# Nine matmuls on zeros at the start, the first norm's column sums one step later, and another count for GpSimd's low parts

## The chip, the core and the metric

The kernel runs on one core of one Trainium2 chip. The metric is the device time of one execution in microseconds, as the median of several runs. A profiled execution gives the trace; its span runs from the first to the last instruction.

## The reference

The kernel computes two transformer blocks in f32 on 256 tokens of width 1024. What matters here is the beginning of the first block:

```python
def rms_norm(x, g):
    xf = x.astype(jnp.float32)
    y = xf * lax.rsqrt(jnp.mean(xf * xf, axis=-1, keepdims=True) + EPS)
    return (y * g.astype(jnp.float32)).astype(x.dtype)

h = rms_norm(x, attn_pre_norm)
proj = h @ w_in                  # queries, keys, values of three attentions, and gates
...                              # attentions, gated merge, w_out, residual
x = x + rms_norm(h, attn_post_norm)
h = rms_norm(x, ffn_pre_norm)
h = conv_ffn(h, w_up, conv_w, conv_b, w_down)
x = x + rms_norm(h, ffn_post_norm)
```

A second block of two layers follows: a modulation made from `ada_w`, a state-space branch, a differential attention and an MLP, with a context stream beside it, and a last `rmsnorm`.

## The kernel before

Activations lie transposed: eight tiles `x[k]` of 128 channels by 256 tokens. A weight comes in pieces of 128x1024 f32 (512 KB). `wload` loads a piece into `wr`, ScalarE rounds it to a high part `wh` (L210), and VectorE or GpSimd subtracts to get the low part `wl` (L213). A product is then three matmuls for each of the eight channel tiles: high by high (L230), high by low of the activation (L231), low of the weight by high (L232), so 24 for a piece. In `mmN` (L251 to L253) the activation is the stationary operand. There are seven `wr` buffers, five `wh` and five `wl`; the program has 578 pieces. Which engine makes a low part is decided by a count:

```python
self.nsplit += 1
eng = nc.gpsimd if self.nsplit % self.pool_every == 0 else nc.vector
```

`pool_every` is 4 for the first block and changes by stage (4, 8 or 99). `nsplit` starts at 0.

A planner puts the instructions of VectorE, ScalarE, GpSimd and the load queue in order, by priority among what is ready by its own estimates. TensorE's order is the one in which the program issues its matmuls (`in_order`). `weave` takes one step of the dense work, then one step of each background generator in `bg`.

The first block begins with the loads of piece 1 (on GpSimd's queue), the eight `x[k]`, and pieces 2 to 4, all of the highest priority. `xg` is `x` times `pre_g` (the tile tag is `o`), split into a high half by ScalarE (L391) and a low half by VectorE (L392). The first dense work, `prods_c`, multiplies `xg` instead of the normed `h`, and applies the norm's factor to the products. Its steps are piece 1, piece 2, piece 3, piece 4 (24 matmuls each), the first half of pieces 5 and 6, their second half. Behind the first half it issues four VectorE products (L489) that use `rt`, the norm's factor spread over the partitions. `prods_b` follows and is the first that needs `h`.

In the background `pre_norm` runs. Its first step squares `x` on GpSimd (`sq`, L299) and adds the squares on VectorE (L303). The next step issues the column sums on TensorE (L312: four plain f32 matmuls, two records each) and the factor `rr` with its diagonals `dg` (L272 to L278: VectorE, GpSimd, VectorE). The next issues `spread` (L286) and `rt` (L405), and the last issues the sweep that makes `h`: `hv` (L410) on VectorE, its high half on ScalarE (L256) and its low half on VectorE (L257). `bias_rows` and, later, `heads_c` and `steps_ada` (L916) run beside it.

`norm` has a `wait` argument: so many more steps go by before the column sums are issued. It is 0 in `pre_norm`.

Of the kernel before, what the change touches and what calls it, by code (L numbers as in the profile page):

```python
# [10 lines left out]
F32 = mybir.dt.float32  # L11
# [6 lines left out]
P = 128  # L18
# [80 lines left out]
class Net:  # L99
    def __init__(self, ctx, tc, A, stop=None, x_only=False):  # L100
        self.ctx, self.tc, self.nc, self.A = ctx, tc, tc.nc, A
        self.stop = stop
        p = lambda name, bufs, **k: ctx.enter_context(tc.tile_pool(name=name, bufs=bufs, **k))
        self.cp = p("cp", 1)
        self.NR, self.NH = 7, 5
        self.back = 4
        self.wr = p("wr", self.NR)
        self.wh = p("wh", self.NH)
        self.wl = p("wl", 5)
        self.ps_mm = p("psmm", 3, space=PSUM)  # L110
        self.ps_sm = p("pssm", 3, space=PSUM)
        self.ps_lg = p("pslg", 2, space=PSUM)
        self.sp = p("sp", 2)
        self.nsplit = 0
        self.HP = 100
        self.MW = 2
        self.H2 = 256
        self.XP = (1,3,5)
        self.GN = 4
        self.RP = 100  # L120
        self.pieces = []
        self.first = None
        self.pv = (4,4,4,8,99,4,4)
        self.pool_every = self.pv[0]
        self.FD = ({2:(0,),4:(1,),6:(2,),7:(3,)},{2:(0,),4:(1,),7:(2,3)})
        self.B0 = (5,5)
        self.WW = ((2,0,1),(2,0,2))
        self.NA = 12
        self.L = (3,2)
        self.L0 = (4,4)  # L130
        nc = self.nc
        self.cst = self.cp.tile([P, 6 * P], F32, name="cst")
        self.smt = self.cp.tile([P, NSM], F32, name="smt")
        self.row = self.cp.tile([P, NRW], F32, name="row")
        self.nhalf = self.cp.tile([P, 4], F32, name="nhalf")
        nc.vector.memset(self.nhalf, -0.5)
        warm = self.cp.tile([P, 4], F32, name="warm")
        nc.scalar.activation(warm, self.nhalf, AF.Copy)

    def constants(self, first):  # L140

        nc, A = self.nc, self.A
        if first:
            for a, b in ((5 * P, 6 * P), (0, P)):
                nc.sync.dma_start(self.cst[:, a:b], A["cst"][:, a:b])
            return
        nc.sync.dma_start(self.smt[:, 8:], A["small"][:, 8:])
        nc.sync.dma_start(self.cst[:, P:5 * P], A["cst"][:, P:5 * P])
        nc.sync.dma_start(self.row, A["rows"].rearrange("(o n) -> o n", o=1).to_broadcast([P, NRW]))
# [191 lines left out]
    def first_block(self, es_x):  # L341


        nc, tc, A = self.nc, self.tc, self.A
        w_in = A["w_in"]
        xsrc = lambda k: A["xT"][k * P:(k + 1) * P, :]
        with ExitStack() as es:
            px = self.side_pool(es_x, "x1", 1, "left")
            with tc.high_priority():
                nc.sync.dma_start(self.smt[:, :8], A["small"][:, :8])  # L350
                early = [self.wload(w_in[0], eng=nc.gpsimd)]
                x = self.load_x(px, xsrc, "xl")
# [41 lines left out]
            bc = []  # L394
# [3 lines left out]
            def pre_norm():  # L398
                t1 = lambda: p4.tile([P, 256], F32, tag="t1", name="hv")
                sq = []  # L400
                for c in range(4):
                    t = pb.tile([P, 2, 256], F32, tag=f"gate{c}", name="sq")
                    sq += [t[:, 0, :], t[:, 1, :]]
                yield from self.norm(x, lambda: sq.pop(), bc, start=True)
                nc.scalar.activation(rt, bc[0], AF.Copy)  # L405
                nc.vector.tensor_copy(rc, bc[1][:, 0:2])
                yield
                for k in range(8):
                    v = t1()
                    nc.vector.scalar_tensor_tensor(v, x[k], self.sm("pre_g", k), rt, op0=ALU.mult, op1=ALU.mult)  # L410
                    self.split(h[k][0], h[k][1], v)
# [260 lines left out]
            with self.in_order():  # L672
                bg += [pre_norm(), bias_rows()]
                self.weave(prods_c(), bg)
                self.ada_init(self.side_pool(es_ada, "ada0", 1, "right"))
                self.constants(False)
                bg += [heads_c(), steps_ada()]
                self.weave(prods_b(), bg)
                nc.vector.tensor_scalar(bg1, self.sm("b_gate"), 0.5, None, op0=ALU.mult)
                bg += [heads_b(0), heads_b(1)]  # L680
                self.weave(prods_a(), bg)
                bg += [heads_a(0), heads_a(1)]
                for c in range(12):
                    self.weave(prod_gates(c), bg)
                while bg:
                    self.step(bg)
            self.dump("d_o", [t for pr in o for t in pr])
            x = self.load_x(px, xsrc, "xl")
# [1169 lines left out]
```

## Time and profile before

| | |
|---|---|
| median of three runs | 2646.24 us (2635.65 to 2649.19) |
| profiled execution, its own time | 2649.53 us |
| its span | 2647.7 us |
| mean granted TensorE clock | 0.986 |
| TensorE matmul busy | 2528.0 us, 95% |
| VectorE, ScalarE, GpSimd busy | 1932.7, 1424.1, 877.6 us |

Busy times are sums over the span. In timeline rows the columns are start, duration, engine, line, operation, output<-input with shapes, count, and in brackets the idle time before the row with what ended it. Matmuls are pipelined: their records overlap, and the distance between starts is the pace.

### The profile page before, as it was taken

The numbers are of one execution on the slowest core, as the hardware profiler recorded it, in microseconds if no ns is written. First come the engines' busy times: TensorE is split into PE (matmuls) and PEld (weight loads), VectorE is DVE, ScalarE is ACT, GpSimd is POOL, SyncE is SP. The second block draws the span as 40 slices with busy tenths as digits, with TensorE's granted clock in tenths as the row PEclk, the third lists the DMA queues.
The fourth block names the chain that finished last, engine by engine and source line by source line (L and its number), as shares of the span: only waits on it lengthen the run. The fifth ranks groups of instructions, "written<-read, shape, count | busy, mean of one in ns | idle before, by whom it ended". The sixth has DMA issues, their size and how long they took to land.

```text
span 2647.7 us, 44610 instructions
## 1 busy us (share of the span) xinstructions
PE 2528.0 (95%) x16698; PEld 2275.9 (86%) x16698; DVE 1932.7 (73%) x3056; ACT 1424.1 (54%) x2722; POOL 877.6 (33%) x757
## 2 busy tenths in 40 slices
PE   7999988999999999999999999999999999999998
PEld 7899988998878888888888977789878888899998
DVE  7887799765666766687646899945777767767664
ACT  5654554554655656576424623235575546665654
POOL 3123532323356556211123310114265543213221
PEclk9999999999999999999999999999999999999999
DMA  7675666654333334332534566524443344356552
GB/s 269 220 229 191 234 211 230 216 190 165 122 120 120 128 120 163 114 107 80 187 127 158 183 215 220 192 97 137 147 160 121 119 157 137 104 170 203 173 188 92
DMA packets 179767, 431.28 MB, mean 163 GB/s; under 512 B 18884, under 2 KB 84610, under 8 KB 179294
## 3 DMA queue, kind: packets, MB, share of 16 engines
q1 hardware_dynamic: 176254, 424.26, 47.9%
q0 software_dynamic: 2720, 3.64, 0.5%
q8 instruction: 132, 2.16, 0.3%
q14 instruction: 85, 0.70, 0.1%
q10 hardware_dynamic: 576, 0.52, 0.1%
HBM read 406.82 MB, written 18.32 MB: 161 GB/s over the span
## 4 chain that ended last, share of the span: by engine, by line
PE 51%; DVE 17%; issue 10%; POOL 8%; ACT 7%; DMA 6%; SPq 1%; POOLq 0%; DVEq 0%; ACTq 0%
PE mm L230 13%; PE mm L231 13%; PE mm L232 13%; DVE th L916 4%; DVE wl L213 4%; PE mm L251 2%; PE mm L252 2%; PE mm L253 2%; DMA wa<-in_adaT_dram 2%; DMA Et<-csd 2%; ACT wh L210 2%; ACT E L1164 1%; POOL E L1172 1%; POOL wl L213 1%; DVE acc L828 1%
## 5 line engine op out<-in xcount | busy, mean ns | idle before, releaser
L210 ACT ACTIVATE wh<-wr 128x1024 fp32r<-128x1024 f32 x578 | 610.3, 1057 | 665.9 <-PE mm L231 556.2
L230 PE MATMUL mm<-h,wh 128*128 128x256 f32 (+1 forms) x2232 | 767.1, 344 | 11.9 <-ACT r L1632 3.5
L213 DVE TENSOR_TENSOR wl<-wr,wh 128x1024 fp32r<-128x1024 f32 x466 | 618.0, 1328 | 217.0 <-ACT wh L210 208.7
L231 PE MATMUL mm<-h,wh 128*128 128x256 f32 (+1 forms) x2232 | 744.0, 333 | 2.8 <-DVE h L946 1.4
L232 PE MATMUL mm<-h,wl 128*128 128x256 f32 (+1 forms) x2232 | 745.7, 334 | 0.0
L213 POOL TENSOR_TENSOR wl<-wr,wh 128x1024 fp32r<-128x1024 f32 x112 | 290.3, 2592 | 798.3 <-ACT wh L210 742.2
L230 PEld LDWEIGHTS mm<-h,wh 128*128 128x128 f32 x2232 | 423.3, 190 | 61.5 <-issue 6.9
L231 PEld LDWEIGHTS mm<-h,wh 128*128 128x128 f32 x2232 | 423.5, 190 | 51.8 <-issue 5.7
L232 PEld LDWEIGHTS mm<-h,wl 128*128 128x128 f32 x2232 | 422.9, 189 | 43.4
L916 DVE SCALAR_TENSOR_TENSOR th<-wa,cb 128x1024 bf16<-128x1024 f32 x192 | 264.6, 1378 | 21.6 <-DMA wa<-in_adaT_dram 19.7
L230 PE MATMUL mm<-mid,wh 128*128 128x256 f32 (+1 forms) x832 | 257.3, 309 | 12.4 <-DVE xc L1732 10.5
L231 PE MATMUL mm<-mid,wh 128*128 128x256 f32 (+1 forms) x832 | 256.4, 308 | 1.4 <-DVE mid L257 1.3
L232 PE MATMUL mm<-mid,wl 128*128 128x256 f32 (+1 forms) x832 | 256.4, 308 | 0.5 <-DVE wl L213 0.5
L251 PE MATMUL mm<-wh,h 128*128 128x256 f32 (+1 forms) x704 | 202.5, 288 | 1.4 <-DVE xl L1732 1.0
L230 PE MATMUL mm<-o,wh 128*128 128x256 f32 x592 | 171.8, 290 | 27.9 <-DVE acc L828 17.4
L252 PE MATMUL mm<-wl,h 128*128 128x256 f32 (+1 forms) x704 | 197.6, 281 | 0.0
L253 PE MATMUL mm<-wh,h 128*128 128x256 f32 (+1 forms) x704 | 197.4, 280 | 0.0
L230 PEld LDWEIGHTS mm<-mid,wh 128*128 128x128 f32 x832 | 157.7, 190 | 23.1 <-issue 11.7
L232 PE MATMUL mm<-o,wl 128*128 128x256 f32 x592 | 170.9, 289 | 3.3 <-DVE wl L213 3.3
L231 PE MATMUL mm<-o,wh 128*128 128x256 f32 x592 | 170.5, 288 | 0.0
L231 PEld LDWEIGHTS mm<-mid,wh 128*128 128x128 f32 x832 | 157.3, 189 | 10.4 <-DVE mid L257 2.0
L232 PEld LDWEIGHTS mm<-mid,wl 128*128 128x128 f32 x832 | 157.8, 190 | 9.2 <-DVE wl L213 0.9
(371 smaller groups left out, 4893.8 us busy)
## 6 DMA issues: line engine op xcount, KB each, us to landing
wr<-in_w_in_dram SPq DMA_DIRECT2D x247, 512.0 KB, 3.7
wr<-in_w_mlp_dram SPq DMA_DIRECT2D x144, 512.0 KB, 4.2
wa<-in_adaT_dram SPq DMA_DIRECT2D x96, 512.0 KB, 4.5
wr<-in_w_up_dram SPq DMA_DIRECT2D x64, 512.0 KB, 4.4
wr<-in_w_out_dram SPq DMA_DIRECT2D x32, 512.0 KB, 3.5
wr<-in_w_down_dram SPq DMA_DIRECT2D x32, 512.0 KB, 4.2
wr<-in_w_ssd_o_dram SPq DMA_DIRECT2D x32, 512.0 KB, 3.7
E<-csd SPq DMA_DIRECT2D x24, 512.0 KB, 4.3
```

The source lines that it names most:

```text
L210: nc.scalar.activation(hi, raw, AF.Copy)
L213: eng.tensor_tensor(lo, raw, hi.bitcast(F32), op=ALU.subtract)
L230: nc.tensor.matmul(ps, wh, xh, start=start and k == 0, stop=False)
L231: nc.tensor.matmul(ps, wh, xl, start=False, stop=False)
L232: nc.tensor.matmul(ps, wl, xh, start=False, stop=stop and k == n - 1)
L251: nc.tensor.matmul(ps, xh, wh, start=k == 0, stop=False)
L252: nc.tensor.matmul(ps, xh, wl, start=False, stop=False)
L253: nc.tensor.matmul(ps, xl, wh, start=False, stop=k == n - 1)
L828: nc.vector.scalar_tensor_tensor(a[:, s:], u[:, :256 - s], cw[:, ch * 3 + tap:ch * 3 + tap + 1], a[:, s:], op0=ALU.mult, op1=ALU.add)
L916: nc.vector.scalar_tensor_tensor(self.junk, raw, 0.5, self.cb[:, s, :], op0=ALU.mult, op1=ALU.mult, accum_out=self.mods[l][:, 2 * i + m, s ...
L1164: nc.scalar.activation(v, v, AF.Exp, bias=ncs[:, 2 * sg + c, i:i + 1])
L1172: nc.gpsimd.tensor_tensor(v, v, t, op=ALU.add)
```

## The change

`__init__` gets a tile of zeros, taken from the `wl` buffers: VectorE clears 128x256 elements, and TensorE multiplies them nine times into a PSUM tile that nobody reads. The tile is plain f32, so these products are of the kind of the column sums and not of the rounded kind of the weights. `pre_norm` calls `norm` with `wait=1`: the column sums are issued behind piece 3 instead of piece 2, `spread` behind piece 4 instead of piece 3, and the sweep that makes `h` behind the first half of pieces 5 and 6 instead of piece 4. `nsplit` starts at -1, which moves the count of every piece of the program by one.

```diff
-        self.nsplit = 0
+        self.nsplit = -1
...
         nc.scalar.activation(warm, self.nhalf, AF.Copy)
+
+        none = self.wl.tile([P, 8, P], F32, tag="wl", name="none")[:, :2, :].rearrange("p a b -> p (a b)")
+        nc.vector.memset(none, 0.0)
+        with self.in_order():
+            ps = self.sm_ps()
+            for _ in range(9):
+                nc.tensor.matmul(ps[:, :256], none[:, :P], none, start=True, stop=True)
...
-                yield from self.norm(x, lambda: sq.pop(), bc, start=True)
+                yield from self.norm(x, lambda: sq.pop(), bc, start=True, wait=1)
```

## Rows read from the trace of the kernel before

**Rows 1.** The page's first line.
```profile
span 2647.7 us, 44610 instructions
```

**Rows 2.** Stretches: busy us of PE, PEld, DVE, ACT, POOL; granted clock, DMA share, GB/s.
```profile
10.00:15.00 5.00, 5.00 (x25) 4.94 (x25) 5.00 (x9) 3.18 (x3) 1.87 (x3) 1.00 0.93 358
...
20.00:25.00 5.00, 5.00 (x32) 5.00 (x31) 2.98 (x6) 0.00 (x0) 0.72 (x1) 0.66 1.02 401
```

**Rows 3.** Timeline of TensorE's matmuls, 9 to 40 us.
```profile
9.20 0.58 PE L232 MATMUL mm<-o,wl 128*128 128x256 f32 x1 [0.90 <-DVE wl L213]
...
9.58 0.41 PE L230 MATMUL mm<-o,wh 128*128 128x256 f32 x1
9.79 0.41 PE L231 MATMUL mm<-o,wh 128*128 128x256 f32 x1
...
14.83 0.28 PE L230 MATMUL mm<-o,wh 128*128 128x256 f32 x1
14.94 0.28 PE L231 MATMUL mm<-o,wh 128*128 128x256 f32 x1
...
19.45 0.83 PE L312 MATMUL sm<-cst,sq 128*128 128x1 f32 x6 [1.90 <-DVE sq L303]
...
21.65 0.41 PE L230 MATMUL mm<-o,wh 128*128 128x256 f32 x1
...
24.93 0.40 PE L230 MATMUL mm<-o,wh 128*128 128x256 f32 x1
...
35.68 0.36 PE L230 MATMUL mm<-h,wh 128*128 128x256 f32 x1 [1.05 <-ACT sl L494]
...
38.65 0.70 PE L613 MATMUL sm<-sl,sl 64*128 64x256 f32 x2
39.19 0.38 PE L614 MATMUL sm<-sl,sl 64*128 64x128 f32 x2
```

**Rows 4.** Timeline of VectorE (DVE), 7 to 34 us.
```profile
7.48 1.66 DVE L213 TENSOR_TENSOR wl<-wr,wh 128x1024 fp32r<-128x1024 f32 x1 [0.46 <-ACT wh L210]
9.07 3.88 DVE L392 SCALAR_TENSOR_TENSOR o<-xl,smt,o 128x256 fp32r<-128x256 f32 x6
...
13.21 1.22 DVE L213 TENSOR_TENSOR wl<-wr,wh 128x1024 fp32r<-128x1024 f32 x1
14.34 1.09 DVE L303 TENSOR_TENSOR sq<-sq 128x256 f32<-128x256 f32 x3
...
16.48 2.92 DVE L303 TENSOR_TENSOR sq<-sq 128x256 f32<-128x256 f32 x2
...
21.32 0.48 DVE L278 TENSOR_SCALAR dg<-cst,rr 128x128 f32<-128x128 f32 x2 [0.84 <-POOL rr L274]
...
30.46 3.40 DVE L410 SCALAR_TENSOR_TENSOR hv<-xl,smt,rt 128x256 f32<-128x256 f32 x3
```

**Rows 5.** Timeline of ScalarE (ACT), near 25 us.
```profile
25.24 0.39 ACT L405 ACTIVATE rt<-sm 128x256 f32<-128x256 f32 x1 [5.76 <-PE sm L286]
```

**Rows 6.** Timeline of GpSimd (POOL), 6 to 20 us.
```profile
6.04 5.83 POOL L299 TENSOR_TENSOR sq<-xl 128x256 f32<-128x256 f32 x7 [1.82 <-DMA xl<-in_xT_dram]
15.04 4.08 POOL L213 TENSOR_TENSOR wl<-wr,wh 128x1024 fp32r<-128x1024 f32 x1 [3.17 <-ACT wh L210]
```

**Rows 7.** Two longer stretches, columns as in the second group.
```profile
80.00:250.00 170.00, 169.54 (x1299) 156.20 (x1298) 138.64 (x258) 95.28 (x186) 40.20 (x21) 1.00 0.65 216
...
300.00:500.00 200.00, 173.41 (x1386) 170.10 (x1386) 185.85 (x278) 98.82 (x161) 67.91 (x42) 0.96 0.67 222
```

**Rows 8.** Low parts of all (min/median/max ns); groups from 300 to 500 us (busy, mean ns).
```profile
L213 POOL TENSOR_TENSOR wl<-wr,wh x112: 2349/2408/5831, 15.0 to 2618.2; 128x1024 fp32r<-128x1024 f32 x112
...
L916 DVE SCALAR_TENSOR_TENSOR th<-wa,cb 128x1024 bf16<-128x1024 f32 x48 | 73.8, 1538 | 2.5 <-DMA wa<-in_adaT_dram 2.2
L213 DVE TENSOR_TENSOR wl<-wr,wh 128x1024 fp32r<-128x1024 f32 x42 | 64.0, 1534 | 0.0
...
L213 POOL TENSOR_TENSOR wl<-wr,wh 128x1024 fp32r<-128x1024 f32 x14 | 38.6, 2756 | 26.0 <-ACT wh L210 23.0 <-PE mm L232 1.5 <-PE mm L231 1.5
```

## The prediction

> **What bounds the kernel now.** I read the page first: the span is 2647.7 us in an execution of 2649.53 us [rows 1], so 1.8 us lie around it. The median of the runs is 2646.24 us, 3.3 below this execution; I make the sum against the execution and carry the difference to the median. The stretches come next. From 80 to 250 us TensorE is busy 169.54 of 170 us: its matmuls, in the order written by hand, set the pace there, so what the opening saves or loses before 80 us is handed on. From 300 to 500 us it is busy 173.41 and VectorE 185.85 of 200 [rows 7]: there VectorE paces.
>
> Then the opening, instruction by instruction. TensorE's third matmul waits until 9.20 us for piece 1's low part. After it the matmuls of 256 columns start 0.21 us apart (9.58, 9.79); from 14.83 they start 0.11 to 0.12 apart, and their records are 0.28 long instead of 0.41 [rows 3]. The first pace is that of 1.2 GHz, the second that of 2.4. (The clock column says 1.00 from 10 to 15 us; it shows no event before the first change, so the spacing is what to read. [rows 2]) At 19.45 TensorE has stood idle 1.90 us, waiting for VectorE's sum of squares. At 21.65 the slow records are back, and the stretch 20 to 25 us shows a granted clock of 0.66 [rows 2, 3]. Piece 4's first matmul starts at 24.93, at the fast pace. The first matmul on h starts at 35.68 after 1.05 us of waiting for ScalarE's sl [rows 3].
>
> **The change, part by part.**
>
> *The zeros.* VectorE's new memset follows its first one, and VectorE is idle then. No row shows a memset of this width; it lies between nothing and the 0.36 us of one two-input pass over 256 columns (three in 1.09 us [rows 4]). TensorE starts at about 1.3 us. The zeros are plain f32: one such product of 256 columns shows as two records and holds the engine from 38.65 to 39.19 us, 0.54 at the fast pace [rows 3]. At the slow pace I scale by the spacings, 0.21 to 0.117: 0.97. Nine take 4.9 us if all are fast and 8.7 if all are slow, so they end between 6.2 and 10.0. Since the clock rose during the first real matmuls of the kernel before, I take six slow and three fast, and an end near 8.8. Only two real matmuls could have run by then (piece 1's low part landed at 9.14 [rows 4]), so the zeros cost nothing: the wait for that low part covers them. Without that cover they would cost the 1.4 us from 7.45 to 8.8.
>
> The Trainium skill (FP8 and Floating Point Precision, TensorE Precision Notes) says that true FP32 takes four passes through the array. By it a zero product is four of the plain spacings, 0.47 us fast and 0.85 slow, and the nine end between 5.5 and 9.0 us; the row says 0.54, and I keep the row.
>
> *The count.* The title says GpSimd starts with the fifth piece. The code says otherwise: the count starts at -1, is raised to 0 before the test, and 0 % 4 is 0. GpSimd gets piece 1, then 5, 9 and so on, where it had 4, 8, 12. What piece 1 loses: VectorE made its low part in 1.66 us, from 7.48 to 9.14 [rows 4]. GpSimd's takes 2.41 us (median of its 112) and 2.76 in the mean of the 14 between 300 and 500 us [rows 8], and took 4.08 where VectorE worked beside it [rows 6]. GpSimd is at that moment inside its squares, seven in 5.83 us from 6.04, 0.83 each [rows 6]. The piece's load and high part are issued at the highest priority, so I take it that its low part goes in after the square then running: from 7.7 to about 10.45. The bounds are 9.9 (no wait, 2.41) and, behind all eight squares, 11.87 + 4.08 = 15.95.
>
> Queued behind it on VectorE are the low halves of xg: six took 3.88 us from 9.07 to 12.95 beside the squares [rows 4], 0.65 each. While GpSimd subtracts, VectorE's two-input passes stand still: two adds took 2.92 us beside the 4.08 one, against 0.36 each; three hv took 3.40 [rows 4, 6]. So they start at 10.45 and end between 13.4 (0.49 each) and 14.35 (0.65 each). VectorE's low part of piece 2, next in its order, then ends at 14.6 to 15.6, where it was 14.43 [rows 4].
>
> Piece 1's last matmuls need the last low half of xg: they end at 13.7 to 14.7; before, 9.58 + 21 x 0.213 = 14.05. Piece 2's 24 start with their low part, 24 x 0.117 = 2.8 us, and end at 17.4 to 18.4; before, 14.83 + 21 x 0.117 = 17.3. So the fast clock is worth nothing here: both pieces wait for VectorE. Up to this point the change loses 0.1 to 1.1 us.
>
> *The column sums a step later.* Piece 3 follows at once; the 1.90 us of idle time goes, and its matmuls run at the fast pace: it ends at 20.2 to 21.2. The column sums take 0.83 us [rows 3], to 21.0 to 22.0. What they need is less late than piece 3: GpSimd's remaining five squares end at 10.45 + 5 x 0.83 = 14.6, VectorE's six adds are 2.2 us, and it also makes the low parts of pieces 3 and 4, 1.22 each. GpSimd's low part of piece 5 may hold the adds to about 21; that is the upper end. Piece 4 then ends at 23.8 to 24.8, the two products of spread (half of 0.54 each) at 24.4 to 25.4. Spread does not wait: from the sums' end to dg's end were 1.5 us [rows 3, 4], and 24 matmuls lie between. Before, the same work ended at 24.93 + 2.8 = 27.7. TensorE is 2.3 to 3.3 us ahead.
>
> Late next is h. rt is done between 25.1 and 26.1, as before (25.63 [rows 5]). The sweep that makes h is emitted a step later, behind the four products with rt: three more passes in front, +1.1. Piece 8's low part comes to VectorE, +1.22, but GpSimd no longer stops the sweep (three hv 3.40 instead of 1.1 to 1.3): -2.1. So h is done by 35.68 + 0.2 = 35.9 at the latest. Its eight parts are used one by one, 0.35 us apart, so the 24 matmuls end by 36.3, where they ended at 35.68 + 2.8 = 38.5. The gain is at least 2.2 and at most TensorE's own 3.3. I take 2.8.
>
> *All later pieces.* GpSimd's 112 low parts [rows 8] all move by one piece, the number stays. Most stand between full TensorE stretches, and there I take nothing. Where VectorE paces, 300 to 500 us, the 42 low parts of VectorE average 1.534 us instead of 1.22 and the 48 ada products 1.538 instead of about 1.22: 13.2 + 15.3 = 28.5 us of standing beside GpSimd's work [rows 8]. The other order may make that a quarter more or less, 7 us either way; I take zero.
>
> Sum: 2649.53 - 2.8 = 2646.7 for an execution like the profiled one, 2643.4 at the median; I say 2643.
>
> **The rivals.**
>
> *A: the low part of piece 1 comes late.* If GpSimd does all eight squares first, it lands at 14.3 to 15.95, and TensorE stands from 8.8 on and falls back to the slow pace as it did at 21.65. For it: in the kernel before all eight squares precede any low part. Against: the piece is emitted first. Piece 1 then ends at 17.1 (fast) to 20.9 (slow, 24 x 0.21), piece 2 at 19.9 to 23.7, and the mark of 27.7 us becomes 27.0 to 30.8: 0.7 faster to 3.1 slower, 2645.5 to 2649.3.
>
> *B, the other side: GpSimd's shifted pieces stop VectorE more where it paces.* Place: 300 to 500 us, 14 low parts. Price: the 28.5 us grow by half, 14.3, less the opening's 2.8: 2657.7. It decides from (13.2 + 2.8) / 14 = 1.1 us more per low part. For it: TensorE idles 27 us there already. Against: number and length of the operations stay. The Trainium skill (SBUF — State Buffer, Who interferes with whom) says that such a VectorE instruction is fully blocked by a GpSimd one that reads SBUF. By it the 14 low parts can block at most their own 38.6 us, which caps the price at 10 if they cause all of the 28.5; the trace agrees that the block is nearly whole, 2.92 us for two adds of 0.36.
>
> *C: the same stretch goes better.* The block falls by 10 us or more, as low parts fall beside matmuls that need VectorE for nothing: 2633 and below.
>
> *D: the words of the title hold,* GpSimd starting with piece 5. Then VectorE's own low part stays at 9.14, pieces 1 and 2 end as before at 17.3, and the gain is 3.2: 2643. The code excludes it; the time would hardly differ.
>
> **How the numbers follow.** My forecast has 0.58, A 0.20, B 0.11, C 0.10, D 0.01. This kernel's runs lie between 2635.65 and 2649.19, so half a per cent, 13.2 us, is about what can be told from no change. Faster than 2633.0 needs most of C and a low median, 0.12; slower than 2659.5 needs B with a high one, 0.07; the rest is 0.81. The range takes the opening's ends (+3 to -3.3), a quarter of the block (7 either way) and the runs' spread (about 5), which do not add up all at once: 2631 to 2656.
>
> **What would show it.** Right: 18 records of zeros between about 1.3 and 9; a GpSimd low part that ends near 10.5; xg's last low half at 13.4 to 14.4; no fall of the clock near 21 us; column sums at 20 to 22 with little idle time before them; the 24 matmuls on h done by about 36. Wrong: a first low part after 12 us, a fall of the clock between 9 and 20 us, or a VectorE stretch from 300 to 500 us whose length changes by more than the opening does. That last would make the forecast wrong most easily.

## The result and the profile after

The changed kernel takes 2660.53 us in the median (five runs, 2658.8 to 2665.51) against 2644.45 for the kernel before in the same set (2635.65 to 2649.19): 1.0069 of it, with an interval of 1.005 to 1.0089. Measured again in another set it gives 1.0067 (1.0043 to 1.009). It is slower by 16 to 19 us where I had forecast 3 faster, and the time lies outside the range.

The profiled execution of the changed kernel has 2665.51 us:

```profile
span 2663.6 us, 44638 instructions
```

That is 15.9 us more of span than [rows 1] and 28 more instructions. From line 139 on, lines stand seven further down: L232 has become L239, L213 is L220, L916 is L923, L634 is L641, L312 is L319.

TensorE's timeline over the opening and beyond, beside [rows 3]:

```profile
1.22 6.39 PE L145 MATMUL sm<-none 128*128 128x256 f32 x18 [1.22 <-DVE none L141]
7.52 0.39 PE L237 MATMUL mm<-o,wh 128*128 128x256 f32 x1
7.74 0.28 PE L238 MATMUL mm<-o,wh 128*128 128x256 f32 x1
9.96 0.39 PE L239 MATMUL mm<-o,wl 128*128 128x256 f32 x1 [1.94 <-POOL wl L220]
15.55 0.39 PE L239 MATMUL mm<-o,wl 128*128 128x256 f32 x1 [0.82 <-DVE wl L220]
22.47 0.83 PE L319 MATMUL sm<-cst,sq 128*128 128x1 f32 x6 [1.16 <-DVE sq L310]
26.05 0.61 PE L293 MATMUL sm<-dg,cst 128*128 128x128 f32 x4
33.11 0.28 PE L237 MATMUL mm<-h,wh 128*128 128x256 f32 x1
36.45 0.38 PE L238 MATMUL mm<-h,wh 128*128 128x256 f32 x1 [1.31 <-DVE h L264]
58.30 1.11 PE L522 MATMUL sm<-pt,sl 128*64 128x256 f32 x2 [6.31 <-ACT pt L642]
149.39 0.45 PE L553 MATMUL sm<-cst,L 128*128 128x128 f32 x1 [3.42 <-DVE L L548]
```

The opening goes much as described, and ends only a little ahead: the first matmul on h is 2.57 us earlier, but after the gap of 1.31 at 36.45 the lead is 1.1 us. The last two lines are what was not foreseen. At 58.30 TensorE has stood 6.31 us, waiting for pt: VectorE adds a head's mask to its scores (L641), ScalarE takes the exponential (L642), and TensorE multiplies the result with the values. At 149.39 it has stood 3.42, waiting for another attention's L, which VectorE scales at the end of a softmax (L547, L548; the scaled logits, below). The same two matmuls in the kernel before:

```profile
55.09 0.65 PE L515 MATMUL sm<-pt,sl 128*64 128x256 f32 x2 [1.42 <-ACT pt L635]
139.22 0.30 PE L546 MATMUL sm<-cst,L 128*128 128x128 f32 x1
```

There TensorE waited 1.42 us for pt, and between 120 and 160 us it waits nowhere.

VectorE and GpSimd in the opening, beside [rows 4] and [rows 6]:

```profile
0.90 0.27 DVE L141 MEMSET none<- 128x256 f32 x1
7.90 6.05 DVE L399 SCALAR_TENSOR_TENSOR o<-xl,smt,o 128x256 fp32r<-128x256 f32 x6 [0.86 <-ACT o L398]
13.87 1.63 DVE L220 TENSOR_TENSOR wl<-wr,wh 128x1024 fp32r<-128x1024 f32 x1
```

```profile
7.54 2.36 POOL L220 TENSOR_TENSOR wl<-wr,wh 128x1024 fp32r<-128x1024 f32 x1 [3.32 <-ACT wh L217]
9.85 6.12 POOL L306 TENSOR_TENSOR sq<-xl 128x256 f32<-128x256 f32 x7
46.96 2.83 POOL L220 TENSOR_TENSOR wl<-wr,wh 128x1024 fp32r<-128x1024 f32 x1 [7.57 <-ACT wh L217]
143.30 2.78 POOL L220 TENSOR_TENSOR wl<-wr,wh 128x1024 fp32r<-128x1024 f32 x1 [12.92 <-ACT wh L217]
```

The last two of these low parts are those of pieces 13 and 33, and each stands just ahead of one of the two long waits. The stretches, columns as in [rows 2] and [rows 7]:

```profile
20.00:25.00 5.00, 3.84 (x35) 3.75 (x34) 4.16 (x10) 1.93 (x2) 1.05 (x2) 1.00 1.02 399
40.00:80.00 40.00, 33.69 (x231) 30.17 (x231) 30.68 (x47) 21.08 (x35) 5.20 (x2) 0.91 0.60 206
80.00:250.00 170.00, 164.83 (x1239) 151.13 (x1238) 132.93 (x246) 95.72 (x188) 33.20 (x18) 0.99 0.65 213
300.00:500.00 200.00, 173.33 (x1365) 170.83 (x1363) 177.36 (x269) 96.74 (x160) 71.22 (x41) 0.94 0.67 227
```

Read against before: from 20 to 25 us the clock now stays up (1.00, it was 0.66). From 40 to 80 TensorE is busy 33.69 us, where it was 38.04. From 80 to 250 it is 164.83, where it was 169.54: the stretch that I called full now has a hole of almost 5 us. From 300 to 500, where I had looked for trouble, TensorE's share is what it was, at a mean granted clock of 0.94 where it was 0.96.

Matching each TensorE matmul with the same one of before gives where the time went (times of the kernel before). The changed kernel is 3.1 us ahead at 24 us, 1.4 at 28, 2.6 at the first matmul on h and 1.1 ahead from 38 to 48; 3.2 behind at 55, 5.7 behind from 59 to 80, 6.7 at 132, 11.6 at 142; then it swings between 10 and 27, losing 1.5 from 300 to 500, and ends 16 behind. More than two thirds of this pair's loss has been made by 150 us.

**The wait at 58 us, instruction by instruction.** VectorE in the changed kernel, 42 to 58 us:

```profile
43.11 0.56 DVE L630 TENSOR_TENSOR s<-s,stick 128x384 f32<-128x384 f32 x1
44.47 0.69 DVE L909 SCALAR_TENSOR_TENSOR cb<-th,cb 128x512 f32<-128x512 f32 x1 [0.79 <-ACT th L908]
45.19 1.22 DVE L923 SCALAR_TENSOR_TENSOR th<-wa,cb 128x1024 bf16<-128x1024 f32 x1
46.34 1.22 DVE L220 TENSOR_TENSOR wl<-wr,wh 128x1024 fp32r<-128x1024 f32 x1
47.48 3.38 DVE L923 SCALAR_TENSOR_TENSOR th<-wa,cb 128x1024 bf16<-128x1024 f32 x1
...
55.98 1.23 DVE L923 SCALAR_TENSOR_TENSOR th<-wa,cb 128x1024 bf16<-128x1024 f32 x1
57.13 0.55 DVE L641 TENSOR_TENSOR pt<-sm,stick 128x384 f32<-128x384 f32 x1
```

and in the kernel before:

```profile
45.18 1.22 DVE L916 SCALAR_TENSOR_TENSOR th<-wa,cb 128x1024 bf16<-128x1024 f32 x1
46.32 2.75 DVE L623 TENSOR_TENSOR s<-s,stick 128x384 f32<-128x384 f32 x1
48.99 1.21 DVE L916 SCALAR_TENSOR_TENSOR th<-wa,cb 128x1024 bf16<-128x1024 f32 x1
...
53.93 0.55 DVE L634 TENSOR_TENSOR pt<-sm,stick 128x384 f32<-128x384 f32 x1
```

What the reader is to see is the queue. s (L630) is a term of the same head's scores that TensorE needs before pt; a conditioning product (L923) is a pass of the modulation made from `ada_w`, whose sums are used only from the stage of the merge on. Between s and pt stand seven conditioning products, a low part and a pass on cb; in the kernel before there are four products between s and pt, since two had been done ahead of s. One product takes 3.38 us instead of 1.22: GpSimd's low part at 46.96 stops it. So s is done 5.4 us earlier than before, at 43.67 instead of 49.07, and pt starts 3.2 later. The long gap costs a second time: from 57 to 63.8 us the granted clock is 0.5, and matmuls start 0.21 us apart again, which turns 3.2 us behind into 5.7.

Most of this is not the count's work. The kernel with zeros and later sums and the count from 0 has six products in the same queue, one of them stopped, waits 5.1 us for pt and is 3.5 behind from 58 to 80 us; as a whole it costs nothing (1.0004, below).

**The wait at 149 us** is the same in small. In the changed kernel the order on VectorE is

```profile
143.87 3.30 DVE L923 SCALAR_TENSOR_TENSOR th<-wa,cb 128x1024 bf16<-128x1024 f32 x1
147.10 0.15 DVE L544 TENSOR_TENSOR st<-st 128x2 f32<-128x2 f32 x1
147.50 0.14 DVE L546 RECIPROCAL rc<-st 128x2 f32<-128x2 f32 x1
147.58 1.19 DVE L923 SCALAR_TENSOR_TENSOR th<-wa,cb 128x1024 bf16<-128x1024 f32 x1
148.71 0.34 DVE L547 TENSOR_SCALAR L<-L,rc 128x256 f32<-128x256 f32 x1
```

A product stopped by GpSimd's low part at 143.30 stands ahead of the softmax's last steps. In the kernel before, GpSimd's low part of the piece before it ran from 132.39 to 134.78 us, ahead of these steps, and there was none beside them. There the last of the scaled logits were ready at 139.07, and TensorE took them at 139.22, so they were in time by 0.15 us. This is the place that belongs to the count: from 138 to 145 us (times of the kernel before) TensorE loses 4.9 us in the changed kernel, 4.7 in its second trace, 4.9 in that of the count alone and 2.5 to 5.0 in the other traces with the first 54 pieces shifted and this piece's low part on GpSimd; it loses 1.3 with this piece back on VectorE, and nothing in the kernels whose first 54 pieces stand as before, with piece 1 moved or not.

### The profile page after: what moved, and what is told of

Same layout as the page of the kernel before. It is cut to its first block, busy times and chain, and to the rows that moved or that the text cites. A ratio compares the mean times of both kernels' runs of the same rounds, so it can differ in the third digit from the quotient of the medians.

```text
span 2663.6 us, 44638 instructions
## 1 busy us (share of the span) xinstructions
PE 2543.3 (95%) x16716; PEld 2287.9 (86%) x16716; DVE 1933.9 (73%) x3057; ACT 1425.7 (54%) x2722; POOL 875.0 (33%) x757
## 4 chain that ended last, share of the span: by engine, by line
PE 47%; DVE 13%; issue 8%; ACT 6%; POOL 6%; DMA 5%; SPq 1%; POOLq 0%; DVEq 0%; ACTq 0%
PE mm L237 12%; PE mm L238 12%; PE mm L239 12%; DVE th L923 4%; DVE wl L220 3%; PE mm L258 2%; PE mm L260 2%; PE mm L259 2%; ACT wh L217 2%; DMA Et<-csd 2%; ACT E L1171 1%; DMA wa<-in_adaT_dram 1%; PE sm L1256 1%; POOL E L1179 1%; DVE cv L1055 1%
## 5 line engine op out<-in xcount | busy, mean ns | idle before, releaser
L220 DVE TENSOR_TENSOR wl<-wr,wh 128x1024 fp32r<-128x1024 f32 x466 | 610.0, 1310 | 224.6 <-ACT wh L217 218.4
L239 PE MATMUL mm<-h,wl 128*128 128x256 f32 (+1 forms) x2232 | 745.6, 334 | 0.0
L220 POOL TENSOR_TENSOR wl<-wr,wh 128x1024 fp32r<-128x1024 f32 x112 | 285.0, 2545 | 854.1 <-ACT wh L217 793.4
L239 PEld LDWEIGHTS mm<-h,wl 128*128 128x128 f32 x2232 | 422.6, 189 | 43.9
L923 DVE SCALAR_TENSOR_TENSOR th<-wa,cb 128x1024 bf16<-128x1024 f32 x192 | 272.4, 1419 | 15.0 <-DMA wa<-in_adaT_dram 13.0
L239 PE MATMUL mm<-mid,wl 128*128 128x256 f32 (+1 forms) x832 | 255.7, 307 | 1.2 <-DVE wl L220 1.2
L239 PE MATMUL mm<-o,wl 128*128 128x256 f32 x592 | 168.9, 285 | 2.8 <-POOL wl L220 1.9
L239 PEld LDWEIGHTS mm<-mid,wl 128*128 128x128 f32 x832 | 157.1, 189 | 10.0 <-DVE wl L220 1.4
```

The lines of the kernel that those rows point to most:

```text
L220: eng.tensor_tensor(lo, raw, hi.bitcast(F32), op=ALU.subtract)
L239: nc.tensor.matmul(ps, wl, xh, start=False, stop=stop and k == n - 1)
L923: nc.vector.scalar_tensor_tensor(self.junk, raw, 0.5, self.cb[:, s, :], op0=ALU.mult, op1=ALU.mult, accum_out=self.mods[l][:, 2 * i + m, s ...
```

## The experiments

My theory after the first reading: the shifted count is the price, through VectorE's queue, in the first 54 pieces as well as later; zeros and later sums cost little. Rivals: piece 1's low part on GpSimd is the price; the later sums are; the zeros are; or any edit makes the planner lay out its queues anew, with a sign of chance. All ratios are to the kernel before in the same set of runs. That kernel's own median moved from 2643.25 to 2650.45 us between sets, so only ratios with their intervals are compared across sets.

**Each part alone.** Count from -1 (no zeros, sums where they were):

```diff
-        self.nsplit = 0
+        self.nsplit = -1
```

> Only the count starts at -1; no zeros, no later column sums. Theory 1 (the shifted count costs: GpSimd's low parts fall beside VectorE products that stand ahead of the softmax work TensorE waits for): 2655 to 2665 us, 10 to 20 above before, with TensorE waits of several us between 50 and 165 us. Theory 2 (the later column sums reorder VectorE's list): within 4 us of before. Theory 3 (any edit makes the planner lay out all four queues anew, the sign is chance): anything within 15 us either way.

Later sums alone:

```diff
-                yield from self.norm(x, lambda: sq.pop(), bc, start=True)
+                yield from self.norm(x, lambda: sq.pop(), bc, start=True, wait=1)
```

> Only the column sums one step later. Theory 1: 2 to 4 us faster than before, since the 1.9 us of idle time and the slow clock behind it go. Theory 2: 8 to 16 us slower, with the long wait of the pv matmuls for ScalarE's pt near 58 us. Theory 3: within 15 us either way.

Zeros alone (the memset and the nine products of the change), and zeros with later sums, the count from 0:

> Only the zeros. Theories 1 and 2: within 3 us of before, since both first pieces wait for VectorE anyhow. Theory 3: up to 10 us either way, if taking a wl buffer and a VectorE memset is enough to change the planner's order.

> The change without its count (which starts at 0 again). Theory 1: 2 to 5 us faster than before, near 2641. Theory 2: as slow as the full change, 2655 to 2665. Theory 3: neither e1 plus this nor the full change need add up.

Measured: count alone 2665.52 us, 1.0056 (1.0036 to 1.0075); later sums alone 2658.63, 1.0018 (1.0004 to 1.0032); zeros alone 2643.58, 0.9973 (0.9959 to 0.9988); zeros and later sums 2651.3, 1.0004 (0.999 to 1.0018). The count carries the price, and it needs neither zeros nor later sums for that. The later sums alone gain 3.8 us by 24 us, as the idle time at 19.45 goes, but give back 1.5 between 35 and 45 and 5.8 between 52 and 58. There the same queue shows, without the shifted count: pt behind six products, one of them stopped.

```profile
46.74 3.27 DVE L916 SCALAR_TENSOR_TENSOR th<-wa,cb 128x1024 bf16<-128x1024 f32 x1
55.01 0.55 DVE L634 TENSOR_TENSOR pt<-sm,stick 128x384 f32<-128x384 f32 x1
```

and TensorE in the same kernel:

```profile
56.17 1.12 PE L515 MATMUL sm<-pt,sl 128*64 128x256 f32 x2 [5.06 <-ACT pt L635]
```

**The queue ahead of pt.** Zeros and later sums, count from 0, with the first conditioning product two steps later:

```diff
                 for i in range(self.NA):
-                    for _ in range(4):
+                    for _ in range(4 if i else 6):
                         yield
```

> Zeros and later column sums, count from 0, and the ada products begin two steps later, so that four instead of six of them stand ahead of pt in VectorE's order. Theory Q (the later column sums lose what they gain because pt stands behind the ada products): the wait for pt near 52 us shrinks by about 2.5 us, and the kernel gains 2 to 4 us on zeros and later sums alone (ratio to before near 0.999). Rival (the loss comes from h being made later): no change of the wait.

Measured 2644.21 us, 0.9978 (0.9961 to 0.9995). Four products stand ahead of pt, pt starts at 53.86, and TensorE waits 2.53 us instead of 5.10; there is no fall of the clock behind it. That is 0.26% below the kernel without this edit, in another set, and the two intervals just overlap. In the traces the edit is worth 3.6 us at 60 us, level with before instead of 3.5 behind: there the queue is what the later sums had lost. The same with 8 in place of 6:

> As the kernel with zeros, later sums and four conditioning products ahead of the first softmax's sum (0.9978 of before, TensorE still waits 2.5 us for it), but with the first of these products two steps later again, so that two stand ahead of it on VectorE. If that queue is all that the later sums had lost at 52 us, the wait shrinks below 1 us and the kernel gains another 1 to 2.5 us, to about 0.997. If the products pushed back are late for the layer's end or meet GpSimd's low parts elsewhere, it stays at 0.998 or above.

Measured 2642.31 us, 0.9994 (0.9978 to 1.001). A miss: the stopped product is still ahead of pt, four stand there and not two, and the wait stays at 2.55. The intervals of the two overlap.

**Piece 1 and the first waits.** The full change with piece 1's low part back on VectorE; then with only the first 54 pieces shifted (where the stage of the merge begins, `self.nsplit += 1` puts the count back); then with pieces 13 and 33, those of 46.96 and 143.30 us, back on VectorE:

```diff
-            eng = nc.gpsimd if self.nsplit % self.pool_every == 0 else nc.vector
+            eng = nc.gpsimd if self.nsplit > 0 and self.nsplit % self.pool_every == 0 else nc.vector
...
+            eng = nc.gpsimd if self.nsplit % self.pool_every == 0 and self.nsplit not in (12, 32) else nc.vector
```

> The full change, but the low part of piece 1 stays on VectorE, so GpSimd really begins with piece 5; all later pieces stand as in the full change. Theory L (the later pieces' shift costs): as slow as the full change, 12 to 18 us above before. Rival F (the first piece's place on GpSimd costs, through the opening): back to zeros and later sums alone, within 4 us of before.

> The full change, with the count put right again after the first block's 54 projection pieces. Theory L1 (the loss is in those projections, 40 to 165 us, beside the softmax work): 8 to 12 us above before. Rival L2 (it is spread over the whole program: 300 to 500, near 740 and near 1900 us): at most 6 us above before.

> The full change, with pieces 13 and 33 on VectorE: the two whose low parts on GpSimd stopped an ada product for 2.1 us each, at 47 and at 143 us. Theory L (the stop decides): the wait for pt near 55 us is 2 us shorter, the wait for the scaled logits near 146 us goes or shrinks to 2 us, and the kernel gains 4 to 7 us on the full change (about 8 to 12 above before). Rival (the planner's new order alone decides): less than 2 us.

Measured: piece 1 back 2659.67 us, 1.0035 (1.0018 to 1.0052); first 54 only 2659.65, 1.0037 (1.0021 to 1.0054); pieces 13 and 33 back 2662.39, 1.0057 (1.0037 to 1.0076). The last shrinks the two waits (6.3 to 3.8 us for pt, 4.7 to 3.5 for the scaled logits) and gains little in the whole: TensorE gets new ones nearby, 1.7 us for s (L630) among them, and at 170 us it is 11.3 us behind, the full change 11.8. It isn't those two low parts alone. I had said that 4 to 7 us gained would speak for the stopped passes and less than 2 for the planner's new order; the two full changes, in other sets, lie some 3 us above, which the intervals do not tell from nothing, so this run decides neither way.

The run with the first 54 shifted shows by chance who sets the time of pt. In its profile the granted clock fell near 39 us:

```profile
38.00:42.00 4.00, 4.00 (x20) 3.82 (x20) 3.61 (x6) 3.95 (x7) 0.84 (x1) 0.60 0.44 127
42.00:46.00 4.00, 4.00 (x21) 4.00 (x20) 2.24 (x4) 3.72 (x5) 0.00 (x0) 0.50 0.87 302
```

By 50 us TensorE had lost 6.4 us against the changed kernel, and yet pt starts as late as in the changed kernel, within 0.3 us, and TensorE does not wait for it:

```profile
57.39 0.55 DVE L641 TENSOR_TENSOR pt<-sm,stick 128x384 f32<-128x384 f32 x1
```

So at 57 us it is VectorE's queue that paces, whatever TensorE does before.

**Is it piece 1's place, and is the price the same elsewhere?** The full change again, piece 1's place alone (count from 0, and `self.nsplit == 1 or` ahead of the test, with zeros and later sums), and two zeros in place of nine:

> The changed kernel once more, so that it stands beside the next three in one set of runs. If its price is the same everywhere, 1.0069 of before as the first time (1.005 to 1.0089). If the part of the price that piece 1's place on GpSimd seemed to have (full change 1.0069, with piece 1 back on VectorE 1.0035) came only from the two being measured on different chips, this run comes out near 1.004.

> Zeros and the later sums, and of the count only what it does to the first piece: piece 1's low part on GpSimd, all later ones (4, 8, 12, ...) where the kernel before has them. If piece 1's place costs by itself, 0.2 to 0.3% (5 to 8 us) above the kernel with zeros and later sums alone (1.0004), so about 1.003. If the price of the count is all in the later pieces that shift, about 1.0004, with a TensorE wait of about 1.9 us for the first low part at 10 us and nothing kept of it later.

> Two products of zeros in place of nine, no other edit. The kernel with nine zeros alone measured 0.9973 of before, with no gain in the opening of its trace. If the gain comes from a TensorE that is already at the higher clock when the first weights land, two products (about 1.4 us) are too few and it falls back to 1.000. If it comes from the mere presence of the memset and of an earlier start, it stays at 0.997. If the 0.9973 was mostly the spread of the runs, both kernels differ from it by about as much as from each other, 0.998 to 1.000.

Measured: the full change 2661.9 us, 1.0067 (1.0043 to 1.009); piece 1 alone on GpSimd 2644.57, 1.0004 (0.9989 to 1.0019), what zeros and later sums give without it; two zeros 2644.2, 1.0001 (0.9984 to 1.0018). Beside zeros and later sums, piece 1's place costs nothing. The wait for its low part stands in that profile (1.8 us at 10), and the opening's lead is smaller by some 2 us at 24, but nothing of it is left further on.

**First pieces and later ones.** Four more, with zeros and later sums in all but the first: nine zeros alone; the count shifted only after the first 54 pieces (`self.nsplit -= 1` where the stage of the merge begins, count from 0); the full change with the first conditioning product four steps later; piece 1 back once more.

> Nine products of zeros alone, as in the run that gave 0.9973. If the zeros gain by themselves, 0.996 to 0.9985 again. If that figure came from the set of runs that it was measured in (its kernel before had a median 6 to 7 us above that of the sets around), it comes out at 0.999 to 1.001, as two products of zeros did.

> Zeros and later sums, with the count as in the kernel before for the first 54 pieces and shifted by one for all that follow: the complement of the run that shifts only the first 54. If the prices add, the full change's 1.0068 less the first 54's 1.0037 and plus the base of 1.0004 gives about 1.0035. If the later pieces cost nothing, as the prediction had it, 1.0004. If all the price is there, 1.0065.

> The full change, with the first conditioning product four steps later, so that two instead of six stand ahead of the first softmax's sum on VectorE. If that queue is the cause of the +5.7 us at 55 to 64 us and what is lost there is kept to the end, the time falls by about 5 to 6 us, to 1.0045 to 1.005. If lost time there is given back later anyway, or the products meet GpSimd's low parts elsewhere, it stays at 1.0068.

> The full change with piece 1's low part on VectorE, as in the run that gave 1.0035, now in a set with others. Since piece 1 alone on GpSimd cost nothing beside zeros and later sums, the reading that its place carries half of the price should fall: 1.006 to 1.007, as the full change. If it is really worth some 8 us in the full change, 1.003 to 1.004 again.

Measured: nine zeros 2644.81 us, 0.9984 (0.9966 to 1.0002); after 54 only 2657.31, 1.0029 (1.0011 to 1.0047); full with later products 2658.72, 1.0039 (1.0023 to 1.0055); piece 1 back 2661.86, 1.0049 (1.0031 to 1.0067).

The two halves of the count add up: 0.33% for the first 54 pieces (1.0037 less 1.0004), 0.25% for the later ones (1.0029 less 1.0004), with the base of 0.04 together 0.62, where the full change has 0.67 and 0.69. Each half carries an uncertainty of some 0.2% from the two intervals that it is taken from. Piece 1 back came out at 1.0035 and 1.0049, between the two values that I had said would decide it, and the full change at 1.0069 and 1.0067. The intervals of all four runs overlap, but the means of the two pairs lie 0.26% apart. Piece 1 alone costs nothing; whether it carries a part of the price in company with the shifted pieces stays open, and if it does, that part sits in the first half. Taking products out of the queue in the full change brings it to 1.0039: 0.3% below the full change in other sets, some 3 us below the neighbour (piece 1 back) in its own set. The sign is the expected one; the size is over the expected 5 to 6 us by the first comparison and under it by the second. Its profile can't be read at pt, because the clock fell at 39 us in it too.

Where the later pieces can cost is seen in the kernel that shifts them alone, though not the sum: its profiled execution has 2.0 us more of span than that of the kernel without the shift (2651.8 and 2649.8). Between 300 and 500 us it loses and gains in steps of up to 3.3 us and stands 7.0 behind the kernel before at either end; it loses 6.4 us from 1900 to 1930, and makes most of that good later. Two of TensorE's waits in its whole trace; the kernel before has none on cv, and 1.2 us in two on yt:

```profile
PE mm L237 <- DVE cv L1056: 2.7, 1, 2.7
PE sm L1283 <- DVE yt L1274: 5.7, 5, 2.6
```

The first is a wait of 2.7 us at a convolution. Both traces of the changed kernel show it too, and the kernel with only the first 54 shifted does not. In the changed kernel it is at 1949.33 us, with these rows of ScalarE ahead of it:

```profile
1938.99 2.45 ACT L1171 ACTIVATE E<-E,ncs 128x128 f32<-128x128 f32 x8 [2.44 <-POOL E L1165]
1941.36 2.44 ACT L1171 ACTIVATE Et<-Et,ncs 128x128 f32<-128x128 f32 x8
1943.70 1.43 ACT L1049 ACTIVATE cv<-mm,cbh,cwh 128x512 f32<-128x512 f32 x2
```

and in the kernel before:

```profile
1916.04 0.76 ACT L1042 ACTIVATE cv<-mm,cbh,cwh 128x512 f32<-128x512 f32 x1
1918.62 2.45 ACT L1164 ACTIVATE E<-E,ncs 128x128 f32<-128x128 f32 x8 [1.82 <-POOL E L1158]
```

No pass is stopped here: VectorE stood idle 6.49 us before its convolution passes, because ScalarE's cv, which they need, now stands behind sixteen other passes, and GpSimd makes no low part between 1906.4 and 1953.9 us. The shifted count has changed the order that the planner gives to ScalarE as well.

That is the rival that the experiments do not take apart. The count moves low parts, and with them it moves the planner's order on every engine; a stopped pass and a new order stand together in both long waits before 150 us. Nor does any run start the count at another value (1 or 2, say), so whether every such move costs this much or only this one stays open.

## Why the prediction was wrong, step by step

**The step that failed is "All later pieces".** I let 112 low parts move by one piece and took nothing for it, because their number and length stay and "most stand between full TensorE stretches". Number and length did stay: GpSimd's 112 low parts take 285.0 us where they took 290.3. What I did not do was to ask of each stretch what stands behind the VectorE pass that a moved low part stops. TensorE's full stretch from 80 to 250 us said that VectorE was in time there, not by how much: the scaled logits were in time by 0.15 us, less than one stopped pass, and for pt TensorE already waited 1.42. The runs put the count at 0.33% for the first 54 pieces and 0.25% for the others, some 9 and 7 us of 2645, where the sum had nothing for either.

**Rival B had a part of the mechanism and the wrong place.** I put the price where VectorE's busy share was highest, 300 to 500 us, as passes stopped there, and gave it 2657.7 us. That this lies near the measured time is luck: the stretch cost 1.5 us and not 14.3. Over half of the price belongs to the first 54 pieces, and in the traces most of theirs arose before 150 us, where VectorE was 17% (40 to 80 us) and 18% (80 to 250 us) idle in the kernel before, and single results came late. As a check on the mechanism over the whole trace, I counted VectorE passes that last over 0.8 us longer than the median of their group while a GpSimd low part runs: 65 before, 118 us above the medians; 74 after, 130 us. That is a tenth more, and the run of the changed kernel in the other set has 72 and 127. The total is far below the half more that I had asked of B. The 12 us would cover most of the loss only if TensorE waited for every one of these passes; what the traces show is a few long waits, in which the order counts as well. The Trainium skill (SBUF — State Buffer, Who interferes with whom) has a VectorE pass with two SBUF inputs contend with a GpSimd instruction that reads SBUF, under an exclusive lock; the trace agrees, with 3.38 us for a product of 1.22 beside a low part of 2.83. Rival B's cap of 38.6 us of low parts from 300 to 500 us was applied to the wrong stretch.

**"What the opening saves is handed on" failed with it.** The lead of 1.1 us was there at 48 us, and 1.7 at 52, and met a result of VectorE that was not ready. The kernel with later sums alone shows that this happens without the count, too: with the sums a step later, s came earlier, and all six products stood between it and pt. That the order on VectorE changes 20 us behind an edit was in neither the sum nor the rivals.

**The opening itself was mis-sized, not misread.** Gain 2.8 predicted, 1.1 measured at 38 us. GpSimd's low part landed at 9.90 (10.45 taken, 9.9 the lower bound), because it went in as soon as its high part was there, behind one square, with no wait for a second. The low halves of xg ended at 13.95 (13.4 to 14.35), VectorE's low part of piece 2 at 15.50 (14.6 to 15.6). The column sums started at 22.47 and ended at 23.3, 1.3 us after the upper end of 22.0, since GpSimd's low part of piece 5 stopped two adds for 2.96 us and another add came behind a low part. The products of spread started at 26.05 where 24.4 to 25.4 was their end, so TensorE was 1.3 us ahead and not 2.3 to 3.3. And h: two hv still stood 3.02 us beside GpSimd (from 31.85), since piece 9's low part stops the sweep now that piece 8's does not. I had taken 2.1 us for an end of that.

**The zeros cost nothing, as said,** and ended at 7.6, not 8.8. One product is two records, and products start 0.85 us apart at the slow pace and 0.43 at the fast one, where I had taken 0.97 and 0.54 from [rows 3]; by the Trainium skill (FP8 and Floating Point Precision, TensorE Precision Notes), which has true FP32 take four passes through the array, the estimate was 0.85 and 0.47, and the trace agrees with the first and is 0.04 under the second. What they buy in the opening, the two traces of nine zeros alone do not agree on: the matmul that the kernel before starts at 67 us is 0.2 us later in one and 1.3 earlier in the other, where the granted clock is 1.00 from 20 to 25 us instead of 0.66. What they are worth in the whole is not settled: 0.9973 and 0.9984 for nine alone, 7.3 us between the kernels with later sums with and without them, 1.0001 for two. In the first of their profiles the kernel with nine pulls ahead in steps of 0.9 to 2.7 us from 490 us on, each where the granted clock fell in the kernel before and not in it. Whether the zeros do that or the executions differ in it, no run here tells.

**Right were** the reading that GpSimd starts with piece 1 and not with piece 5 (it rests on the code; the title above says neither, whatever the prediction makes of a title), that the fall of the clock near 21 us goes, and the sign of the loss that the last sentence of the prediction named as the likeliest way to be wrong, though at another place.

No version here is clearly better than both kernels: zeros with later sums and later products (0.9978 and 0.9994) and zeros alone (0.9973 and 0.9984) lie within 0.3% of before.

## What to carry to other kernels

Here the low parts on GpSimd that moved by one piece kept their own price and changed their victims: for each one that an edit moves, look at which VectorE pass it stops and what queues behind that pass, down to the result that TensorE waits for next. Where one engine is full, look up how early the other engines' results come before calling the stretch safe; 3.2 us of lateness became 5.7 when the clock fell behind the gap. An edit that makes one result earlier, or moves work from one engine to another, can put other work ahead of the next result, on ScalarE as well as on VectorE: follow the order on each engine to the first result that TensorE needs, not only to the end of the edited stage.

## What the runs showed of the hardware

The granted clock can fall in one execution and not in another of the same instructions. In the second trace of the changed kernel it is 0.57 in the mean from 12 to 16 us, in the first 1.00 from 10 to 15 us. In the run with the first 54 pieces shifted TensorE stood 1.3 us up to 36.84, was busy again, and from about 39 us had a granted clock of 0.5 with 4.00 of 4.00 us busy (rows above), until about 52 us. The full change with later products shows the same, and the second run with piece 1 back does from 37 us on. In the changed kernel the same gap of 1.31 us at 36.45 is followed by a clock of 1.00 from 38 to 42 us. One such fall moved TensorE by 6.4 us, which is why the prices above rest on medians and not on single traces.

The same kernel before had medians of 2644.45, 2650.45, 2650.31, 2643.25 and 2648.22 us in the five sets of runs, so a comparison of medians across sets can be off by 0.2 to 0.3% for reasons that no edit has.
